# A two-layer encoder trunk on one core: the end of a scan group forms its result in another tile and reloads its inputs one by one

## The chip, the cores and the metric

The kernel runs on one core of a Trainium2 chip. The metric is the device time of one execution in microseconds; lower is better. Names of engines: TensorE (PE; its weight loads are PEld), VectorE (DVE), ScalarE (ACT), GpSimd (POOL) and SyncE (SP), whose queue issues the DMAs.

## The reference

Two request groups (512 tokens of width 1024 each) go through two layers with shared weights. Layer 0 is RWKV-7 time mixing with a forward and a backward scan; layer 1 is neighbourhood attention on a grid. All is float32. Only the end of layer 0's branch concerns the change:

```python
r = heads(lerp(0) @ w_r); k = heads(lerp(1) @ w_k); v = heads(lerp(2) @ w_v)
z = xn @ w_z
for d in range(2):                     # forward, backward
    ...                                # decay, a, k_d, kk from small low-rank products
    ys.append(_wkv7_scan(r, decay, k_d, v, -kk, kk * a, reverse=(d == 1)))
    bonus.append(jnp.sum(r * k_d * r_k_h, axis=-1, keepdims=True) * v)
y = ys[0] + ys[1]
y = (y - mean) * lax.rsqrt(var + LNX_EPS) * lnx_w + lnx_b      # per head of 64
y = y + bonus[0] + bonus[1]
out = y * jax.nn.silu(z)
return out @ w_o
```

## The kernel before

Activations lie transposed, 128 channels (two heads) by 512 tokens in a tile. A column is one 128x512 result of a projection; it is the sum of eight products, and a product is three matmuls (L802, L803, L804), since weights and activations are split into a high and a low part. ScalarE makes the high part of a weight (L721) and VectorE the low part (L723).

The scan phase is the middle of the program, from 170 to 1186 us of the profile. It handles eight groups one after the other: a request and a set of four heads, `(s, pb)` in the code. A group is prepared (`prep`: gates, decays, the tile `ab`, Gram matrices at L951), its triangular blocks are inverted on VectorE by elimination steps (L994 and L996, 30 of each) and on TensorE (L1025, L1027), then eight chunk steps run the scan (L1068 to L1230). Its end is `finish`: the sums of the scan, `y`, are normalized (L1254 to L1270), and then each half `g` of the group, 128 channels, is completed:

- L1277: a matmul of `ks` with a block of 0.5s gives the bonus sums in a PSUM bank `bp`;
- L1279: VectorE multiplies them with `v`, in the tile `bv`;
- L1285: TensorE transposes half of `y` into another PSUM bank, `yt`;
- L1288: VectorE scales that and adds `bv`, into `bv`;
- L1290: VectorE adds a bias and multiplies with the gate `sz` (from z), into `bv`;
- L1291: `bv` is saved to DRAM as `dy`, and `fetch` (L1244) loads `ks`, `bv` and `sz` for half 1.

Each of the tiles `ks`, `bv` and `sz` has a single buffer. A load into one of them waits for whatever still reads it, a save among them. The next group's half 0 loads the same tiles.

The projections that remain in this phase (r, v, k, r, v and z of the two requests, `w_o` of request 0, the rest of z, and the first 24 columns of the attention's input projection) are the filler: 640 products in that order. The columns of `w_o` may begin when four groups are finished, as they read `dy`.

The order on TensorE, VectorE and ScalarE is written out when the program is built. Every part is a generator, a `Thread`, that yields the engine of its next step, a condition that must hold, and a function that tells when the step's inputs are ready by a build-time clock:

```python
yield "P", free, lambda c: max(room(c), need(ks)(c))
```

`weave` (L1596) always takes the step that can start now and has the best rank (`finish` has rank 4, products 9); a step whose inputs come later by that clock is passed over for others. A step without such a function counts as ready when the thread's step before has ended. Where TensorE would idle, `weave` may put a warming matmul (L1622), whose result is not used. Each engine works through its order without skipping. SyncE is not in that order: its DMAs are ordered by the framework's scheduler. After the scan phase, attention and the output projections follow.

Of the kernel before, what the change touches and what calls it, by code (L numbers as in the profile page):

```python
# [14 lines left out]
ALU = mybir.AluOpType  # L15
# [4 lines left out]
P = 128  # L20
T = 512
D = 1024
# [28 lines left out]
class Clock:  # L51
# [40 lines left out]
    def room(self, key, bufs):  # L92
        s = self.slots.get(key, ())
        return 0.0 if len(s) < bufs else min(self.left(n) for n in s)
# [135 lines left out]
class Trunk:  # L230
# [1006 lines left out]
    def finish(self, s, pb, y):  # L1237

        nc, sp = self.nc, self.sp
        vt, gps, act = nc.vector, nc.gpsimd, nc.scalar  # L1240
        ft = lambda tag: self.t(tag, (P, T), 1, F32, self.front)
        loads = {}

        def fetch(g):  # L1244
            p = 2 * pb + g
            loads[g] = [self.load(ft(n), sp[kind, s, p]) for n, kind in (("ks", "ks"), ("bv", "v"), ("sz", "z"))]

        fetch(0)
        need = lambda *xs: lambda c, n=[x.tensor.name for x in xs]: c.at(n)
        yv = y.rearrange("p i g h v -> p (i g h) v")  # L1250
        st = self.t("st", (P, 4, 16), 2, F32, self.front)
        bc = lambda t: t.unsqueeze(2).broadcast_to([P, 16, HD])
        yield "D", None, need(y)
        vt.tensor_reduce(st[:, 0], yv, axis=AX.X, op=ALU.add)  # L1254
        yield "D"
        vt.tensor_scalar(st[:, 1], st[:, 0], -1.0 / HD, None, op0=ALU.mult)
        yield "D"
        vt.tensor_tensor(yv, yv, bc(st[:, 1]), op=ALU.add)
        for j in (0, 8):
            yield "A"  # L1260
            sq = ft("sq").rearrange("p (j v) -> p j v", j=8)
            act.activation(sq, yv[:, j:j + 8], AF.Square)
            yield "D"
            vt.tensor_reduce(st[:, 2, j:j + 8], sq, axis=AX.X, op=ALU.add)
        yield "A"
        act.activation(st[:, 3], st[:, 2], AF.Sqrt, scale=1.0 / HD, bias=self.eps[:, 1:2])
        yield "D"
        vt.reciprocal(st[:, 3], st[:, 3])
        yield "D"
        vt.tensor_tensor(yv, yv, bc(st[:, 3]), op=ALU.mult)  # L1270
        free, room = self.bank()
        for g in range(2):
            p = 2 * pb + g
            ks, bv, sz = loads[g]
            yield "P", free, lambda c: max(room(c), need(ks)(c))
            bp = self.p("pm")
            nc.tensor.matmul(bp, self.bones, ks, start=True, stop=True)  # L1277
            yield "D"
            vt.tensor_tensor(bv, bp, bv, op=ALU.mult)  # L1279
            yield "P", free, lambda c: max(room(c), need(y)(c))  # L1280
            yt = self.p("pm", (P, NCH, L))
            for i in range(4):
                c0, c1 = (7 - i, i) if i % 2 == 0 else (i, 7 - i)
                o = yt[:, c0:c1 + 1:c1 - c0] if c1 > c0 else yt[:, c0::c1 - c0][:, 0:2]
                nc.tensor.transpose(o, y[:, i, g].rearrange("p h v -> p (h v)"), self.ident)  # L1285
            yield "D"
            ytf = yt.rearrange("p c t -> p (c t)")
            vt.scalar_tensor_tensor(bv, ytf, self.dv[:, 72 + p:73 + p], bv, op0=ALU.mult, op1=ALU.add)  # L1288
            yield "D"
            vt.scalar_tensor_tensor(bv, bv, self.dv[:, 80 + p:81 + p], sz, op0=ALU.add, op1=ALU.mult)  # L1290
            self.save("y", s, p, bv)  # L1291
            if g == 0:
                fetch(1)


    def ht(self, p):
# [340 lines left out]
    def scan_phase(self, mid):  # L1637
# [60 lines left out]
        def each(f):  # L1698
# [5 lines left out]
            Thread(lambda: 1, each(self.outer)),  # L1704
            Thread(lambda: 0, fetch()), Thread(lambda: 0, fetch_x()), *self.flow(), Thread(lambda: 5, inverse()), Thread(lambda: 1.5, preps()),
            Thread(lambda: 1.3 if did["finish"] == 3 else 4, finish()), Thread(lambda: 1.2, self.norm0(0))]
        e = mybir.EngineType
        with self.tc.manual_schedule(engines={e.PE, e.DVE, e.Activation}):
# [202 lines left out]
```

## Time and profile before

| | us |
|---|---|
| median of 3 runs | 1689.23 |
| lowest and highest run | 1682.6, 1691.78 |
| profiled execution | 1683.88 |
| its span, first to last instruction | 1682.1 |
| TensorE busy | 1570.9 |
| VectorE busy | 1227.8 |
| ScalarE busy | 984.0 |

The mean granted TensorE clock was 0.971. The profile covers one execution. A line of the timeline reads: start and duration in us, engine, source line, operation, out<-in by the program's tile names, size; in brackets the idle time of the engine ahead of it and what ended it. A line of the grouped view reads: the same names, count, busy us, mean ns, idle us ahead. The name of a DMA is its target and source; `dv`, `dz`, `dks` and `dy` are in DRAM.

### The profile page before, as it was taken

The numbers are of one execution on the slowest core, as the hardware profiler recorded it, in microseconds if no ns is written. First come the engines' busy times: TensorE is split into PE (matmuls) and PEld (weight loads), VectorE is DVE, ScalarE is ACT, GpSimd is POOL, SyncE is SP. The second block draws the span as 40 slices with busy tenths as digits, with TensorE's granted clock in tenths as the row PEclk, the third lists the DMA queues.
The fourth block names the chain that finished last, engine by engine and source line by source line (L and its number), as shares of the span: only waits on it lengthen the run. The fifth ranks groups of instructions, "written<-read, shape, count | busy, mean of one in ns | idle before, by whom it ended". The sixth has DMA issues, their size and how long they took to land.

```text
span 1682.1 us, 46291 instructions
## 1 busy us (share of the span) xinstructions
PE 1570.9 (93%) x18818; PEld 1201.2 (71%) x18818; DVE 1227.8 (73%) x2725; ACT 984.0 (58%) x1977; POOL 24.1 (1%) x94
## 2 busy tenths in 40 slices
PE   7989898899989998989998999999999899999998
PEld 6767666676766776767765767777777687777776
DVE  8985668688777697887888887865576856555564
ACT  5443655676655667755674665454577655555562
POOL 0000000000000000000000000000000000000000
PEclk9989999899999999999997999999999999999999
DMA  5435678678586786876776665554774347555553
GB/s 209 163 125 187 203 243 261 202 228 257 170 262 211 225 255 205 259 243 205 241 232 214 202 199 199 184 178 131 267 231 155 111 127 249 182 157 175 164 181 107
DMA packets 240821, 336.26 MB, mean 200 GB/s; under 512 B 53696, under 2 KB 119360, under 8 KB 240608
## 3 DMA queue, kind: packets, MB, share of 16 engines
q1 hardware_dynamic: 240608, 333.31, 61.6%
q8 instruction: 148, 2.42, 0.6%
q14 instruction: 65, 0.53, 0.1%
HBM read 227.71 MB, written 105.51 MB: 198 GB/s over the span
## 4 chain that ended last, share of the span: by engine, by line
PE 67%; DVE 11%; DMA 9%; ACT 8%; issue 4%; SPq 1%; DVEq 0%; POOL 0%; ACTq 0%; POOLq 0%
PE pm L802 7%; PE pg L423 6%; PE pg L424 6%; PE pg L425 6%; PE pm L804 5%; PE pm L803 5%; PE pf L1090 2%; PE sc L1433 2%; PE us L1209 2%; DMA cab<-dab 2%; PE po L1466 2%; PE pt L1451 2%; PE zy L1162 2%; PE us L1189 2%; PE zy L1213 1%
## 5 line engine op out<-in xcount | busy, mean ns | idle before, releaser
L802 PE MATMUL pm<-act,whi 128*128 128x512 f32 x640 | 287.6, 449 | 16.1 <-ACT act L771 7.2
L804 PE MATMUL pm<-act,wlo 128*128 128x512 f32 x640 | 256.7, 401 | 12.2 <-DVE wlo L723 12.2
L803 PE MATMUL pm<-act,whi 128*128 128x512 f32 x640 | 258.0, 403 | 5.1 <-DVE act L749 4.2
L423 PE MATMUL pg<-act,whi 128*128 128x512 f32 x448 | 182.4, 408 | 5.9 <-ACT act L372 5.5
L424 PE MATMUL pg<-act,whi 128*128 128x512 f32 x448 | 178.1, 398 | 0.1
L425 PE MATMUL pg<-act,wlo 128*128 128x512 f32 x448 | 177.5, 396 | 0.0
L802 PEld LDWEIGHTS pm<-act,whi 128*128 128x128 f32 x640 | 122.6, 192 | 63.8 <-issue 16.1
L372 ACT CAST whi<-raw 128x512 fp32r<-128x512 f32 x148 | 91.4, 619 | 129.3 <-PE pg L424 75.3
L804 PEld LDWEIGHTS pm<-act,wlo 128*128 128x128 f32 x640 | 123.4, 193 | 44.3 <-DVE wlo L723 16.9
L373 DVE TENSOR_TENSOR wlo<-raw,whi 128x512 fp32r<-128x512 f32 x148 | 101.4, 687 | 70.2 <-ACT whi L372 63.0
L803 PEld LDWEIGHTS pm<-act,whi 128*128 128x128 f32 x640 | 123.6, 193 | 29.6 <-DVE act L749 7.2
L723 DVE TENSOR_TENSOR wlo<-raw,whi 128x512 fp32r<-128x512 f32 x160 | 108.7, 684 | 42.9 <-ACT whi L721 39.5
L721 ACT CAST whi<-raw 128x512 fp32r<-128x512 f32 x160 | 98.1, 616 | 51.7 <-PE pm L803 14.5
L423 PEld LDWEIGHTS pg<-act,whi 128*128 128x128 f32 x448 | 84.8, 190 | 24.8 <-ACT act L372 6.1
L425 PEld LDWEIGHTS pg<-act,wlo 128*128 128x128 f32 x448 | 84.8, 189 | 17.9 <-issue 0.8
L424 PEld LDWEIGHTS pg<-act,whi 128*128 128x128 f32 x448 | 84.9, 190 | 17.4 <-issue 2.0
L996 DVE TENSOR_TENSOR N<-etmp,N 128x30 f32<-128x30 f32 (+14 forms) x240 | 78.5, 327 | 4.2
L994 DVE TENSOR_TENSOR etmp<-N 128x30 f32<-128x30 f32 (+14 forms) x240 | 78.3, 326 | 4.2
L1444 DVE CUSTOM_DVE_ANT_0 sb<-sc,bias 128x256 f32<-128x256 f32 x128 | 49.2, 419 | 31.1 <-PE pt L1451 23.5
L1090 PE MATMUL pf<-cab 64*64 64x128 f32 (+1 forms) x2048 | 67.9, 268 | 2.2 <-issue 2.1
L1447 ACT ACTIVATE sb<-sb,mx 128x256 f32<-128x256 f32 x128 | 63.9, 504 | 9.1 <-DVE mx L1446 9.0
L1113 DVE TENSOR_TENSOR AK<-zy,cc 128x256 f32<-128x256 f32 x63 | 26.6, 421 | 53.5 <-PE zy L1068 51.6
(389 smaller groups left out, 3389.7 us busy)
## 6 DMA issues: line engine op xcount, KB each, us to landing
dab<-ab SPq DMA_DIRECT2D x32, 1024.0 KB, 5.5
cab<-dab SPq DMA_DIRECT2D x64, 512.0 KB, 4.4
raw<-in_w_in_dram SPq DMA_DIRECT2D x128, 256.0 KB, 3.3
bias<-in_rpb_dram SPq DMA_DIRECT2D x32, 384.0 KB, 4.8
raw<-in_w_z_dram SPq DMA_DIRECT2D x32, 256.0 KB, 4.5
dz<-tmp SPq DMA_DIRECT2D x32, 256.0 KB, 3.0
raw<-in_w_k_dram SPq DMA_DIRECT2D x32, 256.0 KB, 4.0
dk<-tmp SPq DMA_DIRECT2D x32, 256.0 KB, 2.2
```

Of the source, the lines that this page charges most:

```text
L372: self.nc.scalar.copy(hi, src)
L373: (eng or self.nc.vector).tensor_tensor(lo, src, hi.bitcast(F32), op=ALU.subtract)
L423: nc.tensor.matmul(ps, hi, x[k][0], start=(k == 0), stop=False)
L424: nc.tensor.matmul(ps, hi, x[k][1], start=False, stop=False)
L425: nc.tensor.matmul(ps, lo, x[k][0], start=False, stop=(k == KT - 1))
L721: nc.scalar.copy(hi, raw[h])
L723: nc.vector.tensor_tensor(lo, raw.pop(h), hi.bitcast(F32), op=ALU.subtract)
L802: nc.tensor.matmul(ps, hi[:, at], xh, start=(k == 0), stop=False)
L803: nc.tensor.matmul(ps, hi[:, at], xl, start=False, stop=False)
L804: nc.tensor.matmul(ps, lo[:, at], xh, start=False, stop=(k == KT - 1))
L996: vt.tensor_tensor(N[:, q + 1:, :q], tv, N[:, q + 1:, :q], op=ALU.add)
L1090: end = nc.tensor.matmul(st.f[half(a), h, 0, d, g] if st.last else st.f[half(a), h, :, d, g], ab[half(h), d, g, 2 * e[d] + 1 - a], rt if s ...
```

## The change

The result is now formed in the tile of `sz`, and the save reads that. `ks` of half 1 is loaded behind the matmul of half 0, `bv` behind the last VectorE instruction of half 0, and `sz` behind the save. The first matmul of a half is ready, by the build-time clock, half a microsecond after `bv` has landed, and two VectorE steps name the tiles that they read.

```diff
-        def fetch(g):
-            p = 2 * pb + g
-            loads[g] = [self.load(ft(n), sp[kind, s, p]) for n, kind in (("ks", "ks"), ("bv", "v"), ("sz", "z"))]
-
-        fetch(0)
+        def fetch(n, kind, g):
+            loads[n, g] = self.load(ft(n), sp[kind, s, 2 * pb + g])
+
+        fetch("ks", "ks", 0)
+        fetch("bv", "v", 0)
+        fetch("sz", "z", 0)
...
-            ks, bv, sz = loads[g]
-            yield "P", free, lambda c: max(room(c), need(ks)(c))
+            ks, bv, sz = (loads[n, g] for n in ("ks", "bv", "sz"))
+            yield "P", free, lambda c: max(room(c), need(ks)(c), need(bv)(c) + 500.0)
             bp = self.p("pm")
             nc.tensor.matmul(bp, self.bones, ks, start=True, stop=True)
-            yield "D"
+            if g == 0:
+                fetch("ks", "ks", 1)
+            yield "D", None, need(bp, bv)
             vt.tensor_tensor(bv, bp, bv, op=ALU.mult)
...
-            yield "D"
-            vt.scalar_tensor_tensor(bv, bv, self.dv[:, 80 + p:81 + p], sz, op0=ALU.add, op1=ALU.mult)
-            self.save("y", s, p, bv)
+            yield "D", None, need(bv, sz)
+            vt.scalar_tensor_tensor(sz, bv, self.dv[:, 80 + p:81 + p], sz, op0=ALU.add, op1=ALU.mult)
+            self.save("y", s, p, sz)
             if g == 0:
-                fetch(1)
+                fetch("bv", "v", 1)
+                fetch("sz", "z", 1)
```

In the changed file the steps of a half have other line numbers: L1277 is now L1278, L1279 is L1282, L1285 is L1288, L1288 is L1291, L1290 is L1293, and the warming matmul L1622 is L1626.

The order of the scan phase changes from the first group's end on, on all three engines. First VectorE at the end of the third group, around the first step of half 1, before (L1279 reads `bv`; `N` and `etmp` are the elimination of the next group, `wlo` a weight's low part):

```order
L994 TENSOR_TENSOR etmp_7001<-N_6999 128x150
L996 TENSOR_TENSOR N_6999<-etmp_7001,N_6999 128x6x25
L994 TENSOR_TENSOR etmp_7001<-N_6999 128x130
L996 TENSOR_TENSOR N_6999<-etmp_7001,N_6999 128x5x26
L1279 TENSOR_TENSOR bv_8241<-pm_8302,bv_8241 128x512
L994 TENSOR_TENSOR etmp_7001<-N_6999 128x108
L996 TENSOR_TENSOR N_6999<-etmp_7001,N_6999 128x4x27
L994 TENSOR_TENSOR etmp_7001<-N_6999 128x84
```

The same place on VectorE in the changed program, up to the last step of half 1:

```order
L994 TENSOR_TENSOR etmp_7092<-N_7090 128x30
L996 TENSOR_TENSOR N_7090<-etmp_7092,N_7090 128x30
L998 TENSOR_TENSOR N_7090<-N_7090,cc 128x1024
L1282 TENSOR_TENSOR bv_8327<-pm_8402,bv_8327 128x512
L1000 MEMSET N_7090 128x32
L723 TENSOR_TENSOR wlo_8410<-raw_8345,whi_8409 128x512
L1291 SCALAR_TENSOR_TENSOR bv_8327<-pm_8415,dv,bv_8327 128x512
L1293 SCALAR_TENSOR_TENSOR sz_8329<-bv_8327,dv,sz_8329 128x512
```

The rest of the elimination now stands ahead of half 1's first step: 19 instructions lie between the end of half 0 and that step, where 12 lay before.

Then TensorE at the end of the fourth group, from the first matmul of half 1 on, before (`act` and `whi`, `wlo` are a product's operands, L872 and L873 belong to the next group's preparation):

```order
L1277 MATMUL pm_10064<-ks_10035,cc 128x512
L872 MATMUL pm_10070<-h_1427_7192,w2h_9821 128x512
L873 MATMUL pm_10070<-h_1427_7192,w2l_9820 128x512
L802 MATMUL pm_10028<-act_9309,whi_9995 128x512
L803 MATMUL pm_10028<-act_9308,whi_9995 128x512
L804 MATMUL pm_10028<-act_9309,wlo_9996 128x512
L802 MATMUL pm_10028<-act_9422,whi_9995 128x512
L803 MATMUL pm_10028<-act_9421,whi_9995 128x512
L804 MATMUL pm_10028<-act_9422,wlo_9996 128x512
L1285 MATMUL pm_10089<-cc,y_8066 128x2x64 x3
L1285 MATMUL pm_10089<-cc,y_8066 128x128
```

And the same place on TensorE in the changed program:

```order
L1278 MATMUL pm_10183<-ks_10101,cc 128x512
L872 MATMUL pm_10191<-h_1478_7484,w2h_9917 128x512
L873 MATMUL pm_10191<-h_1478_7484,w2l_9916 128x512
L1288 MATMUL pm_10198<-cc,y_8167 128x2x64 x3
L1288 MATMUL pm_10198<-cc,y_8167 128x128
L951 MATMUL pf_10208<-ab_10119 32x64 x32
L1626 MATMUL zy_10009<-cc 128x256 x10
L951 MATMUL pf_10295<-ab_10259 32x64 x32
L802 MATMUL pm_10331<-act_10287,whi_10090 128x512
L803 MATMUL pm_10331<-act_10286,whi_10090 128x512
L804 MATMUL pm_10331<-act_10287,wlo_10091 128x512
```

The products that stood here are now placed earlier. The first product shown in the changed program is number 369 of 640, the first one of the `w_o` columns; before, the first product shown was number 349.

## The prediction

> **What bounds the kernel now.** The head of the page came first.
>
> ```profile
> PE 1570.9 (93%) x18818; PEld 1201.2 (71%) x18818; DVE 1227.8 (73%) x2725; ACT 984.0 (58%) x1977; POOL 24.1 (1%) x94
> ```
>
> TensorE is busy for 93% of the span, and a VectorE instruction takes 1227.8/2725 = 0.45 us in the mean. That share is an average, so the table of stretches was asked for the part that holds the groups' ends (columns: stretch, its us, busy us of PE, PEld, DVE, ACT, POOL, then granted clock, DMA share, GB/s).
>
> ```profile
> 400.00:1004.00 604.00, 554.99 (x9643) 416.33 (x9642) 487.46 (x946) 386.61 (x753) 11.88 (x31) 0.96 0.70 223
> 1004.00:1186.00 182.00, 180.88 (x3128) 138.19 (x3128) 125.41 (x248) 88.40 (x164) 3.78 (x4) 0.99 0.55 179
> ```
>
> The ends of the first five groups lie in the first stretch, where TensorE idles for 604 - 555 = 49.0 us. The last three lie in the second, where it idles for 1.1 us: products are left there to fill every pause, so a VectorE stall costs nothing. Next came the waits (engine, tile, line; what was waited for; us in total, times, longest) and, for the third group's end, the chain that ended last (start, us, what).
>
> ```profile
> DVE bv L1279 <- DMA bv<-dv: 18.5, 7, 5.7
> ```
>
> ```profile
> 625.91 5.46 DMA dy<-bv
> 631.39 2.83 DMA bv<-dv
> ```
>
> This is the wait that the change is about. The result of half 0 is saved from `bv`; the load of half 1's `bv` may start only when that save has landed (5.46 us), and lands itself 2.83 us later. VectorE stands at L1279 meanwhile. The timeline of VectorE gives, group by group, the end of half 0 (L1290), the start of half 1 (L1279) and, in brackets, the idle time ahead of it.
>
> ```profile
> 403.63 0.74 DVE L1290 SCALAR_TENSOR_TENSOR bv<-bv,dv,sz 128x512 f32<-128x512 f32 x1
> 413.31 0.69 DVE L1279 TENSOR_TENSOR bv<-pm,bv 128x512 f32<-128x512 f32 x1 [1.40 <-issue]
> 529.05 0.74 DVE L1290 SCALAR_TENSOR_TENSOR bv<-bv,dv,sz 128x512 f32<-128x512 f32 x1
> 540.26 0.69 DVE L1279 TENSOR_TENSOR bv<-pm,bv 128x512 f32<-128x512 f32 x1 [4.49 <-DMA bv<-dv]
> 624.46 0.74 DVE L1290 SCALAR_TENSOR_TENSOR bv<-bv,dv,sz 128x512 f32<-128x512 f32 x1
> 634.34 0.69 DVE L1279 TENSOR_TENSOR bv<-pm,bv 128x512 f32<-128x512 f32 x1 [4.65 <-DMA bv<-dv]
> 738.34 0.75 DVE L1290 SCALAR_TENSOR_TENSOR bv<-bv,dv,sz 128x512 f32<-128x512 f32 x1
> 743.94 0.69 DVE L1279 TENSOR_TENSOR bv<-pm,bv 128x512 f32<-128x512 f32 x1 [0.53 <-DMA bv<-dv]
> 885.40 0.74 DVE L1290 SCALAR_TENSOR_TENSOR bv<-bv,dv,sz 128x512 f32<-128x512 f32 x1
> 894.02 0.69 DVE L1279 TENSOR_TENSOR bv<-pm,bv 128x512 f32<-128x512 f32 x1 [1.80 <-DMA bv<-dv]
> ```
>
> Save and load together thus take 8.9, 10.5, 9.1, 4.9 and 7.9 us from the end of L1290, and VectorE idles for 12.9 us in these five. What TensorE pays is in its own timeline:
>
> ```profile
> 414.06 0.66 PE L1285 MATMUL pm<-cc,y 128*128 128x128 f32 x4 [0.84 <-DVE bv L1279]
> 541.01 0.50 PE L802 MATMUL pm<-act,whi 128*128 128x512 f32 x1 [1.47 <-DVE N L1000]
> 635.09 1.12 PE L1285 MATMUL pm<-cc,y 128*128 128x128 f32 x4 [5.11 <-DVE bv L1279]
> 744.69 0.50 PE L872 MATMUL pm<-h,w2h 128*128 128x512 f32 x1 [0.59 <-DVE bv L1279]
> 897.44 0.79 PE L802 MATMUL pm<-act,whi 128*128 128x512 f32 x1 [4.05 <-ACT act L771]
> ```
>
> In the third group TensorE's queue stood behind the transposes, which need a PSUM bank that L1279 had yet to free. The 541 us pause ends with the memset that VectorE does right after L1279. Of the 4.05 us at 897 us, I put down the 1.80 us that L1279 held VectorE; the rest is the residual chain of x1. The sum is 0.84 + 1.47 + 5.11 + 0.59 + 1.80 = 9.8 us.
>
> **What the change takes away.** All 9.8 us, if the loads are in time, and something more: the long pauses are followed by a lower granted clock.
>
> ```profile
> 520.00:525.00 5.00, 3.98 (x72) 2.50 (x73) 2.79 (x7) 3.98 (x9) 0.00 (x0) 0.66 0.88 266
> 630.00:635.00 5.00, 0.00 (x0) 0.00 (x0) 0.66 (x2) 1.14 (x2) 0.00 (x0) 0.92 0.87 269
> 635.00:640.00 5.00, 4.91 (x14) 4.05 (x15) 4.66 (x13) 0.91 (x2) 0.00 (x0) 0.50 0.32 107
> 640.00:645.00 5.00, 4.50 (x20) 3.31 (x19) 5.00 (x7) 4.01 (x7) 0.00 (x0) 0.90 0.42 121
> 895.00:900.00 5.00, 2.56 (x5) 1.78 (x6) 4.94 (x8) 1.24 (x2) 0.00 (x0) 0.70 0.73 260
> 900.00:905.00 5.00, 5.00 (x61) 3.79 (x61) 4.97 (x6) 2.21 (x3) 0.00 (x0) 0.62 0.98 325
> ```
>
> Behind the third group's end the loss is 5 x (0.08 + 0.50 + 0.10) = 3.4 us, and it goes with the 5.11 us. Behind the fifth it is 5 x (0.30 + 0.38) = 3.4 us, but there 4.05 - 1.80 = 2.25 us of idle stay. A pause of that size had a lower clock behind it elsewhere, in the stretch from 520 us (0.66):
>
> ```profile
> 521.02 1.59 PE L1277 MATMUL pm<-ks,cc 128*128 128x512 f32 x2 [2.50 <-ACT th L876]
> ```
>
> So I count nothing for the fifth, with 3.4 us as the other bound. The Trainium skill (TensorE: Matmul & The Clock Gate, What's actually happening) puts the drop to half after at least one idle window of about 3.4 us; by that, 2.25 us would not drop it and the sum would gain the 3.4 us. The row at 521 us, 2.50 us and yet 0.66, speaks against relying on it.
>
> **What the change adds and moves.** The new gates bind the builder's clock alone, so no instruction waits for more on the chip than its own data. No instruction is added to VectorE or ScalarE; TensorE gets 98 warming matmuls (L1622) for 97. Ten records, which are five instructions since each leaves two, would take ten times 0.23 us by the pace of a product's three matmuls:
>
> ```profile
> 535.47 0.40 PE L802 MATMUL pm<-act,whi 128*128 128x512 f32 x1
> ...
> 536.17 0.60 PE L1285 MATMUL pm<-cc,y 128*128 128x128 f32 x4
> ```
>
> Three matmuls start in 0.70 us, 0.23 us each. A warming matmul of two such passes costs at most 0.5 us: that is the added one.
>
> The SyncE queue:
>
> ```profile
> 398.94 0.33 SPq L328 DMA_DIRECT2D ks<-dks  x1
> ...
> 404.41 0.34 SPq L325 DMA_DIRECT2D dy<-bv  x1
> ...
> 409.83 0.32 SPq L328 DMA_DIRECT2D bv<-dv  x1
> ```
>
> `ks` is already reloaded right behind the matmul that uses it, as SyncE is not ordered by hand; that part of the change I cost at nothing, and below nothing is not in sight either. The queue stood 5 us on `dy` before issuing `bv`, with weight, `rb` and `k` loads behind. Afterwards it issues `bv` at once and stands just as long before `sz`, with one to five loads and saves of the same kinds between: cost nothing, so long as the save lands as fast.
>
> The wait itself moves from L1279 (`bv`) to L1293 (`sz`), since `sz` is now what the save reads. `sz` can land no sooner than `bv` did: 8.9, 10.5, 9.1, 4.9 and 7.9 us. Between the two half-ends VectorE now has 33, 23, 23, 12 and 16 instructions ahead of L1293 (14, 11, 12, 7 and 13 ahead of L1279 before). At 0.45 us that is 14.9, 10.4, 10.4, 5.4 and 7.2 us, which leaves 0.1 us in the second group and 0.7 us in the fifth. Most rows there are elimination steps, shorter than the mean:
>
> ```profile
> L996 DVE TENSOR_TENSOR N<-etmp,N 128x30 f32<-128x30 f32 (+14 forms) x240 | 78.5, 327 | 4.2
> ```
>
> In the third group, 15 of 23 rows are such steps. I take 2 us for what is left, between 0.8 and about 4. `bv` alone needs one transfer, its median being
>
> ```profile
> DMA to landing us min/median/max: 2.9/3.5/4.0
> ```
>
> and has 21, 17, 19, 9 and 11 instructions ahead of it (4 us at least): hidden, unless it takes the 7 us of the 533 us load.
>
> The sum against the profiled execution: 1683.9 - 9.8 - 3.4 + 2.0 + 0.5 = 1673.2 us. The profiled execution lies 5.3 us below the median of the runs shown (1689.23), so the forecast for the median is 1689.2 - 10.7 = **1678.5 us**. The smallest difference that a measurement of this kernel can tell is about 0.5%, 8.4 us.
>
> **The rivals.** (a) The wait only moves. Then the instructions put ahead of L1293 are taken from behind it, and `sz`, landing later because `dy` now shares the engines with `bv`, stalls VectorE there. Each of L1282 and L1291 with what lies between earns perhaps 1.9 us, so waits fall from 12.9 to about 5.3 us. TensorE keeps 9.8 x 5.3/12.9 = 4.0 us and the clock loss of the third group: gain 5.8 us, less 0.5, so 1684 us. For it: the latency is the same; against: the new order has 3 to 19 more instructions ahead of it. 0.25.
>
> (b) Slower: products run dry at the fourth group's end. Counted in the order, 360 products stand ahead of that end (343 before), and 368 ahead of its second L1278 (348): 368 is where the columns of `w_o` begin, and those need the fourth group finished. Before, 20 products of 0.70 us, 14 us, stood behind the second matmul; now there are none, so each us by which VectorE is late to half 1 and to the first `w_o` operand (L749) reaches TensorE. Price: 14 us plus two such clock losses, 6.8, less the 10.7 won, which is +10 us: 1699 us. It decides against the change from some 11 us of new idle there. For it: the order; against: eleven more warming matmuls stand behind it (5 us; ten fewer stand elsewhere), so the builder saw most of the pause, and the scan reaches the fifth end with 435 products done instead of 445, which is work saved for later, not lost. 0.25.
>
> That the change does nothing is no case: both half-ends move in the order.
>
> **How the numbers follow.** The forecast has 0.50. Its low end takes the fifth group's clock (3.4), no wait left (2) and a luckier spread of the 39 us of idle that remain up to 1004 us, of which I allow a quarter, 10 us: 1663. The high end goes most of the way to (b): 1697. Faster by over 0.5%: 0.50; within: 0.25, (a); slower: 0.25, (b).
>
> **What would show it.** Right: `bv` no longer among VectorE's waits, `sz` at L1293 with under 4 us in the first five, no 5 us pause of TensorE or clock of 0.50 after the third end, 39 us idle up to the sixth group. (a): `sz` at L1293 with 5 us or more. (b): a pause of over 5 us between the fourth end and the first `w_o` product. Wrong altogether: idle that grows in stretches without a group's end, or in the stretch after 1004 us.

## The result, and the profile after

| | before | changed |
|---|---|---|
| median of 20 runs each, us | 1689.14 | 1694.16 |
| lowest and highest, us | 1678.9, 1694.29 | 1689.64, 1701.52 |
| ratio, 95% interval | | 1.0035 (1.002 to 1.005) |
| profiled execution, its span, us | 1683.88, 1682.1 | 1691.19, 1689.4 |
| mean granted TensorE clock | 0.971 | 0.971 |

The changed kernel is slower by 0.35%, some 6 us, where 10.7 us of gain were forecast. First its two stretches with group ends (columns as in the prediction: stretch, its us, busy us of PE, PEld, DVE, ACT, POOL, then granted clock, DMA share, GB/s):

```profile
400.00:1004.00 604.00, 553.72 (x9661) 415.01 (x9660) 491.33 (x950) 390.45 (x763) 11.88 (x31) 0.97 0.72 226
1004.00:1186.00 182.00, 178.11 (x3114) 136.24 (x3113) 123.93 (x247) 85.67 (x157) 3.79 (x4) 0.99 0.55 173
```

TensorE idles for 50.3 us in the first (49.0 before; 39 were forecast) and 3.9 us in the second (1.1 before). Yet the wait that the change is about has nearly gone. These are VectorE's waits at the group ends, all that `bv` and `sz` have:

```profile
DVE sz L1293 <- issue: 1.2, 1, 1.2
DVE bv L1282 <- DMA bv<-dv: 1.0, 1, 1.0
DVE bv L1291 <- PE pm L1288: 0.9, 3, 0.4
DVE bv L1282 <- PE pm L802: 0.8, 1, 0.8
DVE bv L1282 <- PE pm L1278: 0.3, 1, 0.3
```

The load of `bv` costs VectorE 1.0 us where it cost 18.5. At the third end, which had the longest pause, half 1 starts without a wait, and the granted clock stays at 1.00 where it fell to 0.50:

```profile
635.81 0.68 DVE L1282 TENSOR_TENSOR bv<-pm,bv 128x512 f32<-128x512 f32 x1
...
637.80 0.75 DVE L1293 SCALAR_TENSOR_TENSOR sz<-bv,dv,sz 128x512 f32<-128x512 f32 x1
```

```profile
630.00:635.00 5.00, 4.89 (x22) 3.41 (x21) 4.66 (x16) 1.33 (x3) 0.00 (x0) 1.00 1.05 323
635.00:640.00 5.00, 4.22 (x20) 3.27 (x21) 4.96 (x9) 2.40 (x6) 0.00 (x0) 1.00 1.00 304
640.00:645.00 5.00, 4.67 (x23) 3.52 (x23) 4.25 (x3) 4.96 (x8) 0.00 (x0) 1.00 0.56 202
```

A loss shows at the next end. TensorE's timeline there, after the change (L1626 is the warming matmul; the profile leaves two records for each):

```profile
743.45 0.40 PE L804 MATMUL pm<-act,wlo 128*128 128x512 f32 x1
743.68 0.60 PE L1626 MATMUL zy<-cc 128*128 128x256 f32 x2
...
744.58 1.02 PE L1278 MATMUL pm<-ks,cc 128*128 128x512 f32 x2
...
746.72 0.86 PE L951 MATMUL pf<-ab 64*32 64x64 f32 x64
747.50 4.58 PE L1626 MATMUL zy<-cc 128*128 128x256 f32 x20
755.21 0.85 PE L951 MATMUL pf<-ab 64*32 64x64 f32 x64 [3.12 <-DVE ab L916]
756.47 0.50 PE L802 MATMUL pm<-act,whi 128*128 128x512 f32 x1 [0.42 <-ACT act L747]
```

The last matmul of product 368 starts at 743.45 us; product 369, the first of `w_o`, starts at 756.47. The second of the next group's two Gram blocks (L951) needs `ab` and comes 8.5 us after the first. Before, some 7 us lay between the two, and nine products filled them:

```profile
746.04 0.86 PE L951 MATMUL pf<-ab 64*32 64x64 f32 x64
...
753.17 0.86 PE L951 MATMUL pf<-ab 64*32 64x64 f32 x64
```

Now no product is left to put between: ten warming matmuls and 3.12 us of idle stand there. Counted over the stage from the fourth end to the fifth (start of the first VectorE reduction of each end; first line: products by their L802, second line: records of warming matmuls, two for each), before:

```profile
724.39:846.91 122.52, 38.53 (x87) 0.99 0.68 220
724.39:846.91 122.52, 5.39 (x22) 0.99 0.68 220
```

And after:

```profile
727.02:844.80 117.78, 29.50 (x65) 0.97 0.66 212
727.02:844.80 117.78, 12.40 (x44) 0.97 0.66 212
```

The stage has 22 products fewer, 15.4 us at 0.70 us each, but is only 4.7 us shorter. With the products taken off it costs 72.3 us instead of 61.6: 10.7 us more. Warming matmuls went from 11 to 22. That this is also the size of the forecast gain is chance. Nor is it the whole account: the stage from the first end to the second, counted the same way, is 7.5 us cheaper after the change, and up to the start of the last product the two profiled executions differ by 1.7 us only.

Behind the scan there is a second loss. From the last product to the end of the program, before and after:

```profile
1179.60:1682.00 502.40, 484.08 (x2748) 381.86 (x2746) 311.56 (x966) 283.92 (x638) 0.00 (x0) 0.99 0.54 175
```

```profile
1181.30:1689.40 508.10, 487.50 (x2742) 383.24 (x2740) 310.02 (x963) 282.55 (x638) 0.00 (x0) 0.98 0.53 172
```

This part is 5.7 us longer, though the change edits nothing in it. Its instructions were dealt anew by the framework's scheduler. TensorE's idle time is 20.6 us there instead of 18.3; the rest of the 5.7 us is busy time (487.50 instead of 484.08).

### The profile page after: what moved, and what is told of

Read it like the earlier page. It is cut to its first block, busy times and chain, and to the rows that moved or that the text cites. A ratio compares the mean times of both kernels' runs of the same rounds, so it can differ in the third digit from the quotient of the medians.

```text
span 1689.4 us, 46296 instructions
## 1 busy us (share of the span) xinstructions
PE 1572.3 (93%) x18820; PEld 1201.0 (71%) x18820; DVE 1229.1 (73%) x2725; ACT 982.1 (58%) x1977; POOL 24.2 (1%) x94
## 5 line engine op out<-in xcount | busy, mean ns | idle before, releaser
L802 PE MATMUL pm<-act,whi 128*128 128x512 f32 x640 | 284.9, 445 | 17.2 <-ACT act L747 4.3
L802 PEld LDWEIGHTS pm<-act,whi 128*128 128x128 f32 x640 | 122.8, 192 | 62.2 <-issue 11.5
L1201 ACT COPY X<-us 64x256 f32<-64x256 f32 x128 | 47.0, 367 | 33.3 <-PE zy L1068 30.1
```

Source lines behind the costliest of these rows:

```text
L802: nc.tensor.matmul(ps, hi[:, at], xh, start=(k == 0), stop=False)
```

## The experiments

Each ratio is against the kernel before, run on the same chip in the same session; 6 to 12 runs each. The kernel before had medians of 1685.02, 1687.4, 1685.21 and 1683.62 us in the four sessions, one for each part below, on three chips. A ratio is not exactly the quotient of the two medians, and where ratios of different sessions are set side by side, that assumes that they carry over from chip to chip.

**1. Data movement and order apart.** Two records were taken while a program is built: what `weave` picks, step by step, and the order of the instructions behind the scan. Either can be forced on another kernel. The first run forces the picks of before on the change: it keeps the new tile, loads and saves, and has before's order on TensorE, VectorE and ScalarE. The order behind the scan then comes out as before's by itself, by its trace; the loop at the end of the edit stands in the other runs, where that order has to be forced, on SyncE too:

```diff
         ck, did = self.clock, self.did
+        for j in _unpack(PICKS):        # the picks of the other kernel, -1 a warming matmul
+            ck.t["P"] = ck.pe()
+            ...
+                threads[j].step()
+        return
         while True:
...
+        for o in (REST_PE, REST_DVE, REST_Activation, REST_SP):
+            o = _unpack(o)
+            for x, y in zip(o, o[1:]):
+                self.tc.add_manual_dep(ins[y], ins[x].name, ...)
```

> The changed data movement (result in the tile of sz, three separate reloads) under the order of before on TensorE, VectorE, ScalarE and GpSimd, written out from a record of it, in the scan phase and after it. If the order lost the time (theory 1), the waits at the group ends shrink here as forecast and nothing is re-dealt: 3 to 10 us faster than before, 1679 to 1686. If the new movement of data itself costs (theory 2: SyncE's queue or shared DMA engines), about as slow as the change, 1694.

Measured: 1680.08 us, ratio 0.9961 (0.9942 to 0.998). The data movement alone is a gain of 0.39%, 6.6 us. The reverse, the kernel before with the change's order everywhere:

> The data movement of before (result in bv, all reloads behind the save) under the order of the change, in the scan phase and after it. Theory 1: as slow as the change or slower, 1694 to 1700, since the order carries the loss. Theory 2: about before, 1686 to 1690.

Measured: 1700.68 us, 1.009 (1.0064 to 1.0117). Taking the new data movement away from the change (1.0035) thus costs 0.55%, so it is a gain in either order. The old wait is back in this run:

```profile
DVE bv L1396 <- DMA bv<-dv: 12.3, 5, 4.8
```

The dear stage goes with the order and not with the data movement: from the fourth end to the fifth, less 0.70 us a product, the first run has 60.4 us and this one 72.6, as before (61.6) and change (72.3) have.

Then the order alone, split in two. The kernel before with only the change's order behind the scan:

> Before, with the stage after the scan (attention, projections) put into the order that it has in the change. Theory 1, where the traces put 6.9 us of loss behind the scan: 4 to 7 us slower than before, 1693 to 1696. If that loss was only this one execution's: no change, 1689.

Measured: 1692.16 us, 1.0037 (1.0019 to 1.0055). And the change with only before's order behind the scan:

> The change, with the stage after the scan put into the order that it has in before. Theory 1: the loss behind the scan goes and the scan nets to nothing, 1687 to 1690, within 0.2% of before. If the scan phase lost the time: still 1694.

Measured: 1686.28 us, 1.001 (0.9992 to 1.0028). The part behind the scan went with its order and not with the scan ahead of it, in the first of these two (old scan, new rest) and in the second (new scan, old rest):

```profile
1176.10:1685.00 508.90, 486.75 (x2748) 382.47 (x2746) 312.22 (x966) 282.87 (x638) 0.00 (x0) 0.99 0.54 173
```

```profile
1185.90:1689.80 503.90, 485.34 (x2742) 383.04 (x2740) 310.10 (x963) 283.80 (x638) 0.00 (x0) 0.98 0.54 173
```

A single trace is weak evidence for this part: over all runs of this document it took 507.5 to 509.2 us in the four traces with the new order, 501 to 507.5 us in those with the old one, and 514.8 us in one of these, the run with `EPS` 70. The ratios carry it better.

So the change is three things: data movement -0.39%, scan order +0.49% (1.001 against 0.9961; 0.37% by the two medians), order behind the scan +0.25% (1.0035 against 1.001). Together that is +0.35% by construction, as the three steps lead from 1 to the measured 1.0035; each part carries about 0.2 to 0.3% of uncertainty. The third has a check of its own in the 1.0037 of the kernel before with the new rest.

**2. Does any newly dealt order cost as much?** Three runs deal the scan order anew without touching the data movement, with the rest order of before. `EPS` is the slack by which a step's inputs may be late and it still counts as startable; `LAT["D"]` is VectorE's latency in the build-time clock.

```diff
-    NZ1, STOCK, EPS, NEAR = 6, 1, 60.0, 400.0
+    NZ1, STOCK, EPS, NEAR = 6, 1, 50.0, 400.0     # and 70.0
...
-    LAT = dict(P=210.0, A=125.0, D=116.0, G=120.0, S=0.0)
+    LAT = dict(P=210.0, A=125.0, D=120.0, G=120.0, S=0.0)
```

> Before, with its data movement and with its order behind the scan, but one number of the builder's clock moved a little (EPS, the time by which a step may be ready later and still be taken, 60 to 50 ns): the scan phase's order is re-dealt as widely as by the change, for no reason of its own. If a re-dealt scan order is in itself what costs (theory 1a: the order of before is a good one among many), 0.2 to 0.8% slower, 1688 to 1698. If the new gates make a bad order of their own (theory 1b, the filler spent early), no change within 0.2%, 1682 to 1688.

> The same with EPS moved the other way, 60 to 70 ns. Theory 1a: 0.2 to 0.8% slower. Theory 1b: within 0.2% of before.

> The same with another number: the latency that the builder's clock gives to VectorE, 116 to 120 ns. Theory 1a: 0.2 to 0.8% slower. Theory 1b: within 0.2% of before.

Measured: 1.0049 (1.0027 to 1.0071), 1.0084 (1.0051 to 1.0117) and 1.001 (0.9993 to 1.0027). The fourth run has the new data movement without the new gates, so that the builder does not know of the loads:

```diff
-            yield "P", free, lambda c: max(room(c), need(ks)(c), need(bv)(c) + 500.0)
+            yield "P", free, lambda c: max(room(c), need(ks)(c))
...
-            yield "D", None, need(bp, bv)
+            yield "D"
...
-            yield "D", None, need(bv, sz)
+            yield "D"
```

> The changed data movement without any of the new gates (the first matmul waits for ks alone, no needs of bv and sz), so that the builder deals an order of its own; the order behind the scan is that of before. Theory 1a: the gain of the data movement (0.4%) against a loss as in the three runs beside it: within 0.4% of before. Theory 1b: as the old order with the new data movement, 0.3 to 0.5% faster.

Measured: 1708.36 us, 1.0129 (1.0103 to 1.0155), far above what either theory gave. Here all 368 products stand ahead of the fourth end, and the pause is at its longest:

```profile
740.17 0.40 PE L896 MATMUL pm<-act,wlo 128*128 128x512 f32 x1
740.41 2.32 PE L1718 MATMUL zy<-cc 128*128 128x256 f32 x10
...
751.48 4.91 PE L1718 MATMUL zy<-cc 128*128 128x256 f32 x22
761.58 1.17 PE L1043 MATMUL pf<-ab 64*32 64x64 f32 x64 [5.19 <-DVE ab L1008]
763.37 0.79 PE L894 MATMUL pm<-act,whi 128*128 128x512 f32 x1 [0.62 <-ACT act L839]
```

Four orders, four prices from nearly nothing to 1.3%: either a lottery or something that these orders share. With `EPS` 50 and without gates all 368 products ahead of `w_o` stand ahead of the fourth end's half 1, as in the change, and these are dear; the next runs act on that place.

**3. Covering the fourth end.** From here on theory b is the prediction's rival (b), that products run dry at the fourth end, and theory a is the lottery (not the prediction's rival (a)). All runs have the rest order of before, and all but one the change's data movement and gates. Two move the place where `w_o` begins, by one and two more columns of z ahead of it:

```diff
-    NZ1, STOCK, EPS, NEAR = 6, 1, 60.0, 400.0
+    NZ1, STOCK, EPS, NEAR = 7, 1, 60.0, 400.0     # and 8
```

> The change with the rest order of before, and NZ1 = 7 instead of 6: one more z column stands ahead of the columns of w_o, so these begin with product 377 instead of 369. At the fourth group's end 360 products stand ahead of its first half and 371 ahead of its second, as in the change (360, 368), but no warming matmul is left between products 368 and 369 (11 in the change), and 93 instead of 98 in the whole scan. Theory b (products run dry at the fourth end): the pause between products 368 and 369 falls from 13.5 us to under 3, the 11 us that the stage from the fourth to the fifth end costs more than in the order of before mostly go, and the kernel gains 5 to 10 us on the change with the rest order of before (1686.3, ratio 1.001): ratio to the kernel before 0.995 to 0.998. Theory a (any newly dealt order costs some 0.5%, wherever): ratio stays at 1.001 or above.

> As the run with one more column, but NZ1 = 8: w_o begins with product 385. The fourth end is covered (360 and 371 products, no warming matmul between 368 and 369), but now the products stand at 454 and 455 at the sixth end with 20 and 12 warming matmuls about it, and 104 in the whole scan. Theory b: the cost of the fourth end goes and a like one comes at the sixth, so the ratio lies near that of the change with the rest order of before, 1.000 to 1.005, and worse than with one more column. Theory a: no relation to where products run dry, anything from 1.001 to 1.008, and no better with one more column than with two.

Measured: 1.001 (0.9986 to 1.0034) and 1.0087 (1.0056 to 1.0118). With one column the pause moved to products 376 and 377, where it is 4.1 us long (6 warming matmuls), but the gain expected did not come. With two there is no pause there, and the ratio is worse than the 1.000 to 1.005 that theory b gave. A dearer stage appears near the place that was expected, from the sixth end to the seventh: products and records of warming matmuls of that stage with two more columns, then in the change with the old rest order:

```profile
940.56:1071.16 130.60, 39.00 (x87) 0.97 0.55 175
940.56:1071.16 130.60, 11.66 (x49) 0.97 0.55 175
```

```profile
974.26:1094.35 120.09, 43.72 (x100) 0.97 0.57 184
974.26:1094.35 120.09, 0.00 (x0) 0.97 0.57 184
```

Less 0.70 us a product, that is 69.7 us against 50.1. The stage ahead of it is cheaper, though (74.3 us against 83.1), and these two profiled executions took 1689.66 and 1691.62 us, so the traces do not show where the 0.9% go. The next two runs hold products back instead, until the fourth group's steps are through: one in the change, one in the kernel before with `EPS` 50 (there from product 348 on).

```diff
-                        "P", lambda: h in w and (g, k) in x and (k > 0 or (free() and c - 2 not in self.post)),
+                        "P", lambda: h in w and (g, k) in x and (8 * c + k < 344 or did["steps"] >= 32) and (k > 0 or (free() and c - 2 not in self.post)),
```

> The change with the rest order of before, and a rule that products from number 344 on wait in the builder until the fourth group's elimination is done: 356 and 360 products stand ahead of the fourth end's halves instead of 360 and 368, so 8 are left for the pause between the second half and the columns of w_o. 5 warming matmuls instead of 11 stand between products 368 and 369, 92 instead of 98 in all. Theory b: the pause from 368 to 369 falls from 13.5 to some 6 us, and the kernel gains 3 to 7 us on the change with the rest order of before: ratio 0.997 to 0.999. Theory a: 1.001 or more.

> The kernel before (its old data movement) with the planner's EPS at 50 instead of 60, which alone gave 1.0049 and a pause of 16.7 us between products 368 and 369, and with products from 348 on held until the fourth elimination is done: 360 and 365 products at the fourth end's halves instead of 362 and 368, 6 warming matmuls instead of 11 between 368 and 369, 97 instead of 94 in all. Theory b: the pause shrinks to some 9 us and the ratio falls from 1.0049 to 1.000 to 1.003. Theory a: it stays within 0.2% of 1.005 or goes up, as it is another newly dealt order with more warming matmuls.

Measured: 1680.42 us, 0.9969 (0.9949 to 0.9989), and 1690.97 us, 1.0033 (1.0012 to 1.0055). The first is what theory b gave, a little better. In the second the pause shrank to 9.3 us; its gain on 1.0049 lies within the intervals and decides nothing. TensorE in the first, with five warming matmuls and no idle between products 368 and 369:

```profile
755.52 0.40 PE L896 MATMUL pm<-act,wlo 128*128 128x512 f32 x1
755.75 2.32 PE L1718 MATMUL zy<-cc 128*128 128x256 f32 x10
758.09 0.50 PE L894 MATMUL pm<-act,whi 128*128 128x512 f32 x1
```

**4. The place, or all filler?** Since one more column won nothing, a third theory was set up, that the price is all of TensorE's idle and warming time in the scan, wherever it lies. The hold with one more column tells them apart, as the builder puts 105 warming matmuls into it. Two more runs repeat the hold in another order, and put the change's rest order behind the hold.

```diff
-    ... (8 * c + k < 344 or did["steps"] >= 32) ...
+    ... (8 * c + k < 348 or did["steps"] >= 32) ...
```

> As the hold from product 344, but from 348: 359 and 365 products ahead of the fourth end's halves, 6 warming matmuls between products 368 and 369, 94 in all, rest order of before. Fourth end (b) and filler (c, TensorE's idle and warming time in the whole scan, 143.6 us with the hold at 344, 149.6 in the change's scan order) say the same here: ratio 0.997 to 1.000. Theory a (any newly dealt order costs about 0.5%): 1.001 or more, the 0.9969 of the other hold was luck.

> The change with products held from number 344, scan order as in that run (0.9969), but with the change's order behind the scan. If the order behind the scan costs its own 0.3% as it did on the kernel before (1.0037) and between the change with its own and with the old rest order (1.0035, 1.001): ratio 0.999 to 1.001, and the part behind the scan 508 to 509 us long instead of 502 to 505. If that cost came from the scan it stood behind: 0.997.

> The change with NZ1 = 7 and products held from number 348, rest order of before: 359 and 365 products ahead of the fourth end's halves, no warming matmul between 368 and 369 (w_o begins with product 377), but 105 warming matmuls in all, 13 of them at the fifth and sixth end more than with the hold alone. Theory b (the fourth end alone decides): ratio 0.995 to 0.999. Theory c (idle and warming time in the whole scan, about 155 us by 105 warming matmuls of 0.8 us and 72 to 76 us of idle): ratio 1.003 to 1.007.

Measured: 1677.61 us, 0.996 (0.9937 to 0.9984); 1681.94 us, 0.9984 (0.9964 to 1.0005); 1675.13 us, 0.9947 (0.9929 to 0.9965). The hold wins in three orders, with no column (0.9969, 0.996 against 1.001) and with one (0.9947 against 1.001). The last has the most warming matmuls of the three and is the fastest, against the third theory in the number that it forecast; in the trace its idle time fell as well, so idle and warming together stayed at 147.6 us and were not the 155 estimated (from 185 to 1176 us; the durations of warming records are added singly, though they overlap). That sum does not put the runs in the order of their times either: it is 144.1 us with one more column, which won nothing, and 146.8 us with the hold from 348, which won 0.5%. The stretch of the fastest run up to 1004 us idles for 43.7 us, and product 377 follows 376 within 1.9 us:

```profile
400.00:1004.00 604.00, 560.25 (x9691) 422.79 (x9690) 493.59 (x958) 390.74 (x761) 11.78 (x30) 0.96 0.72 228
```

The new rest order behind the hold cost 0.15% in the second run (0.25% and 0.37% in the others), within their uncertainty the same. All orders side by side, the pause being from the start of the last product ahead of `w_o` to the first of `w_o`, with other work of TensorE in it, and half 1 the second half of the end:

| run | products ahead of the fourth end's half 1 / of w_o | pause, us (warming matmuls) | ratio |
|---|---|---|---|
| before | 348 / 368 | 0.7 (0) | 1 |
| new movement, old order | 348 / 368 | 0.7 (0) | 0.9961 |
| hold 348, one more column | 365 / 376 | 1.9 (1) | 0.9947 |
| hold 344 | 360 / 368 | 3.0 (5) | 0.9969 |
| hold 348 | 365 / 368 | 3.8 (6) | 0.996 |
| one more column | 371 / 376 | 4.1 (6) | 1.001 |
| change, old rest | 368 / 368 | 13.5 (11) | 1.001 |
| no gates | 368 / 368 | 23.7 (18) | 1.0129 |
| two more columns (dry at 454) | 371 / 384 | 0.8 (0) | 1.0087 |
| old movement, LAT 120 | 362 / 368 | 3.1 (6) | 1.001 |
| old movement, EPS 70 | 364 / 368 | 6.0 (1) | 1.0084 |
| old movement, EPS 50 and hold | 365 / 368 | 9.3 (6) | 1.0033 |
| old movement, EPS 50 | 368 / 368 | 16.7 (11) | 1.0049 |

Two rows do not fit: `EPS` 70, whose loss lies at least in part elsewhere and was not followed (12 us more than before behind the scan in its trace), and one more column without the hold, whose pause is short and which still gained nothing. What that one loses is open. The hold is also more than a cover: it changes which steps stand around the fourth end, and in the stage from the fourth end to the fifth it wins only 2 to 4 us (69.7, 68.9 and 67.6 against 71.6), the rest in other stages; one more column alone won as much there (67.0) and nothing in time. Some of the gain may also be clock: the mean granted clock over all executions was 0.9708 in the change with the old rest order and 0.9720, 0.9715 and 0.9734 with the three holds (the kernel before: 0.971 in these sessions). Shown is that the scan order costs about 0.5% and that holding products there got it back in the three orders tried; that it is the pause of 13.5 us is argued.

## Why the prediction was wrong

- **The wait and its 9.8 us, with the 3.4 us of clock:** right in mechanism. `bv` fell from 18.5 us of wait to 1.0, the clock behind the third end stayed at 1.00. The data movement alone measured 0.39%, 6.6 us, where the sum's net was 10.7: about 4 us less, and 10.7 us lie just outside the interval (3.4 to 9.8 us). One piece is in the trace of the change: the sum takes off all 9.8 us "if the loads are in time", and at the second end the load of `bv` was not. VectorE waited 1.0 us for it, and TensorE 2.39 us behind that:

```profile
536.23 0.50 PE L802 MATMUL pm<-act,whi 128*128 128x512 f32 x1 [2.39 <-DVE bv L1282]
```

Another may be the old order in which the 6.6 us were measured, where VectorE waits longer for the bonus matmul instead (3.4 us before):

```profile
DVE bv L1315 <- PE pm L1311: 7.4, 4, 4.2
```

- **2.0 us for `sz`, 0.5 us for a warming matmul:** bounds held; `sz` waited 1.2 us, and for no load by the profile. The warming matmuls kept TensorE busy for 50.0 us (196 records) against 51.1 (194): nothing.
- **The `ks` part and SyncE at nothing:** no run tells these apart from the rest of the movement, and none shows a cost.
- **The step that failed:** "The sum against the profiled execution" subtracts what leaves the group ends and lets the re-dealt order stand at nothing everywhere else. The order was the larger part: +0.49% in the scan, about 8 us, and +0.25% behind it, about 4 us, against the 6.6 us won.
- **Rival (b)** had the place: 360 and 368 products ahead, a pause there of 13.5 us, the stage 10.7 us dearer; its mechanism is likely and, as said above, not proven. It was held at 0.25 by two reasons that both fell. Eleven warming matmuls did not mean that the builder had covered the pause; they are part of it. And the products done ahead were not all "work saved for later": 22 fewer products shortened the next stage by 4.7 us, not 15.4. Its price was too high: 14 us and two clock losses, 20.8 us together, where the scan order measured about 8. That its 1699 us still lies near the measured 1694 is luck, since some 4 us of those come from behind the scan, where it saw nothing.
- **What no case held:** the program behind the scan is dealt anew too, and cost 0.25%. The prediction looked at the scan alone. Its sign for "wrong altogether", idle that grows "in the stretch after 1004 us", did come, with 2.8 us, but these lie in the scan, ahead of 1181 us; behind the scan it is 2.3 us. Pauses of TensorE behind the scan, first before, then after:

```profile
1340.55 1.22 PE L423 MATMUL pg<-act,whi 128*128 128x512 f32 x2 [5.54 <-ACT act L372]
```

```profile
1337.82 0.73 PE L423 MATMUL pg<-act,whi 128*128 128x512 f32 x2 [1.19 <-ACT act L372]
1343.33 0.80 PE L424 MATMUL pg<-act,whi 128*128 128x512 f32 x1 [4.78 <-DVE act L373]
1347.34 0.80 PE L423 MATMUL pg<-act,whi 128*128 128x512 f32 x1 [1.93 <-ACT os L1494]
```

Where one pause of 5.54 us and one of 0.33 us stood, there are now three, of 7.9 us in all. That is 2 of the 5.7 us; what makes up the others is open.

## What to carry to other kernels

Where an order is dealt by a planner, an edit is two changes: what it does, and the deal that follows. Measure them apart by replaying the old order under the new code; here the edit won 0.4% and the deal lost 0.7%. And filler is a stock: when an edit lets it be used earlier, find where it runs out, count warming instructions as idle time there, and hold some back for the place with the longest chain; with that, one more column ahead, and the old order behind the scan, the same edit came to 0.9947 of the time before.

## What the runs showed of the hardware that was not expected

Two executions of one and the same TensorE order differ by about as much as the change is worth. From 185 to 1176 us, the kernel before and the kernel before with another rest order, which run the same TensorE order there:

```profile
185.00:1176.00 991.00, 918.19 (x15395) 692.16 (x15394) 765.39 (x1479) 609.77 (x1185) 22.27 (x50) 0.97 0.68 217
```

```profile
185.00:1176.00 991.00, 913.03 (x15408) 689.64 (x15407) 766.62 (x1480) 609.89 (x1185) 22.29 (x50) 0.98 0.69 218
```

The granted clock differs by 0.01 and the busy time by 5.2 us. Up to the first group's end the four kernels named next have one TensorE order in their traces, and yet that end came at 383.0 us in the kernel before, 387.1 in the change, 388.0 with the hold from 348 and 380.4 with the hold and one more column. So a difference of a few us in a single profile may be the execution's and not the order's, and a stage is best read from several runs of the same order, as the one behind the fourth end can be.

And an idle of 3.12 us, with 4.58 us of warming matmuls ahead of it, was followed by a lower clock in the changed kernel:

```profile
750.00:755.00 5.00, 2.09 (x10) 1.49 (x8) 3.35 (x8) 1.76 (x4) 0.11 (x1) 1.00 1.01 350
755.00:760.00 5.00, 3.33 (x70) 2.51 (x71) 4.77 (x13) 3.64 (x8) 0.00 (x0) 0.72 0.75 228
760.00:765.00 5.00, 4.66 (x12) 2.97 (x11) 4.83 (x12) 0.62 (x1) 0.00 (x0) 0.60 1.00 305
```

Before, at the same place, an idle of 2.03 us at 754.7 us had a lower clock behind it too, for a shorter time (5 x (0.29 + 0.05) = 1.7 us lost, against 3.4):

```profile
755.00:760.00 5.00, 3.28 (x8) 2.60 (x9) 5.00 (x10) 2.36 (x6) 0.00 (x0) 0.71 1.01 331
760.00:765.00 5.00, 5.00 (x22) 4.08 (x21) 2.47 (x7) 1.01 (x2) 0.00 (x0) 0.95 0.93 287
```

The length of the idle does not settle it, however: in the changed kernel an idle of 2.45 us that ended at 880.62 us had a clock of 1.00 behind it, up to 900 us. What decides is not shown here.
